# Retention groups of a decoder trunk: weight halves two products ahead, two weight sums by adding transfers, another order of groups

## The chip, the cores and the metric

The kernel runs on one core of one Trainium2 chip. TensorE (PE) multiplies matrices, VectorE (DVE) and ScalarE (ACT) do the elementwise work, GpSimd (POOL) a few small operations and some transfers, SyncE (SP) issues most transfers. The metric is the device time of one execution in microseconds (us), as a median of runs; lower is better.

## The reference

A trunk of two layers over 16 meta tokens and 512 tokens of width 1024, all in float32: a retention mixer, a SwiGLU FFN, a gated DeltaNet mixer, a second FFN, with RMS norms before each and a last one. The change lies in the retention mixer, which for each of 4 heads (key width 256, value width 512) computes

```
proj = h @ w_in;  q, k, v, g = split(proj)
q, k = rope(q), rope(k) / 16
scores = (q k^T) * decay mask of the head      (causal, all earlier tokens)
o = scores v
o = o * rsqrt(mean(o^2) + eps) * gn_w * silu(g)
out = concat(o) @ w_out
```

The kernel uses no chunks: it forms the scores of all 528 positions against the meta tokens (padded to 96 rows) and against four tiles of 128 tokens.

## The kernel before, in words

Every float32 product is made of three matmuls of a faster format: an operand is split into a high half (`whi`, a rounding copy on ScalarE) and a low half (`wlo`, a subtraction on VectorE), and `mm3` multiplies high by high, high by low and low by high. All its matmuls carry L407 in the profile, the splits L397/L398 (in `split`) or L170/L171 (in `load_w`).

The projections of head 0's queries and keys and of the gates of heads 0 and 1 are plain products. The other nine projections, named (head, kind) with the kinds QK, V and G, are done as Strassen groups in `quad`: seven products in place of eight, each of 24 matmuls on one of seven prepared combinations of the activations (`forms`: b11, t1, t2, b22, t3, b21, t4; names `fhb`, `fht`, `flb`, `flt` in the profile) and one of seven combinations of the weight blocks. `quad_part` makes the weight combination that the next product needs: it adds blocks on VectorE (L264, four additions per group), loads block "22" a second time, and splits the result. The loads (L257) go through four buffers `wraw`, the halves through three buffers `whi` and `wlo` each. The results are taken out of two PSUM pairs by `taken` (L287 to L304): three of the seven on VectorE, the others on ScalarE. Its destination is one of three row tiles: `at` and `bt` (in the buffer `xlo`) and `ct` (in the buffer `h`, as `oraw`, the attended output).

Beside the groups runs the work of the heads. `rope` rotates queries and keys (L530) with the tile `at` as its scratch; `ret_scores` makes masked scores (L582, L601); `ret_values` transposes values (L618, L626) and splits them; `ret_attend` multiplies (L644, L656), squares and scales (L660 to L665); `row_rsqrt` gives the norm's factor, with a power on POOL (L497) between two small sets of matmuls. `normed` (L781) applies it, `gated` (L800) multiplies by the gate and splits. Finished heads and gates wait in DRAM (`d_o`, `d_sg`) and are reloaded at the end.

The order of the work is written out by hand. A helper is a Python generator; `spawn(gen, delay)` queues it, and `tick()`, called after every second set of three matmuls of a group, runs those that are due. A `yield n` puts off the rest by n ticks, so that a group (28 ticks) interleaves with the helpers. `finish` runs a helper to its end at once. The framework that builds the program then gives each engine and each transfer queue one fixed order by priority and its own reckoning of when operands are there, which follows the written order mostly, not always. Each engine then works through its own queue in order.

The order of the heads is: (0,V); then for each head QK, V and, for heads 2 and 3, G. The rotation of a head is spawned after its QK group and so falls into the V group behind it, over about 16 ticks. After the last group, the three stored heads are gated and split, and the output projection (`w_ro`) starts with head 0.

Of the kernel before, what the change touches and what calls it, by code (L numbers as in the profile page):

```python
# [11 lines left out]
ALU = mybir.AluOpType  # L12
# [18 lines left out]
VT = 3  # L31
# [4 lines left out]
ROPED = 1  # L36
# [14 lines left out]
class Hybrid:  # L51
# [196 lines left out]
    def quad_begin(self, w):  # L248

        q = {"w": w, "raw": {}, "parts": []}  # L250
        for i, n in enumerate(self.BLOCKS):
            self.quad_fetch(q, n, i)
        return q

    def quad_fetch(self, q, n, i):
        q["raw"][n] = self.t(self.wp, [P, 1024], "wraw", bufs=RAW)
        self.nc.sync.dma_start(q["raw"][n], q["w"][i])  # L257

    def quad_part(self, q):

        raw = q["raw"]

        def add(dst, src):
            self.nc.vector.tensor_tensor(raw[dst], raw[dst], raw[src], op=ALU.add)  # L264

        n = len(q["parts"])
        if n in (1, 2, 3):
            add("22", ("21", "11", "12")[n - 1])
        if n == 4:
            add("21", "11")  # L270
            self.quad_fetch(q, "last", 2)
        src = ("11", "22", "22", "22", "21", "12", "last")[n]
        q["parts"].append(self.split_w(raw[src]))

    def quad(self, q, forms, hw, rows, following=None):
# [8 lines left out]
        nq = None  # L284
# [21 lines left out]
        for n, form in enumerate(self.FORMS):  # L306
            if n == 4 and following is not None:
                nq = self.quad_begin(following)
            if n < 6:
                self.quad_part(q)  # L310
            elif nq:
                self.quad_part(nq)
# [5 lines left out]
            for i in range(2):  # L318
                for k in range(4):
                    ws = slice(i * 512 + k * P, i * 512 + (k + 1) * P)  # L320
                    self.mm3(
                        [banks[i]],
                        (hi[:, ws], lo[:, ws]),
                        [(fh[:, k, :], fl[:, k, :])],
                        n in (0, 1, 5) and k == 0,
                        k == 3,
                        skip_group_check=True,
                    )
                    if k % 2:
                        self.tick()  # L330
            taken(n)
# [143 lines left out]
    def row_rsqrt(self, pool, acc, n, out):  # L475
# [27 lines left out]
        for j in range(4):  # L503
            nc.tensor.matmul(  # L504
                pr[:, j * P : (j + 1) * P], rc[:, j + 1 : j + 2].to_broadcast([P, P]), self.ident, start=True, stop=True
            )
        rb = self.t(pool, [P, T], "rb")
# [12 lines left out]
    def rope(self, qk, rows, tmp, cosr, sinr):  # L520
# [3 lines left out]
        r4 = rows.rearrange("p (n s) t -> p n s t", n=2)  # L524
        t1, t2 = r4[:, :, 0, :], r4[:, :, 1, :]
        x1, x2 = tmp[:, 0:2, :], tmp[:, 2:4, :]
        cos, sin = (c.unsqueeze(1).to_broadcast([P, 2, T]) for c in (cosr, sinr))
# [4 lines left out]
        tt(x1, t1, cos)  # L532
        yield ROPE
        tt(x2, t2, sin)
        yield ROPE
        tt(x1, x1, x2, ALU.subtract)
        yield ROPE
        self.split(hi[:, :, 0, :], lo[:, :, 0, :], x1)
        yield ROPE
        tt(t1, t1, sin)  # L540
        yield ROPE
        tt(t2, t2, cos)
        yield ROPE
        tt(t1, t1, t2, ALU.add)
        yield ROPE
        self.split(hi[:, :, 1, :], lo[:, :, 1, :], t1)

    def spread(self, dst, src):
# [5 lines left out]
        )  # L554

    def ret_scores(self, rp, dp, hd, q, k, km, out):
# [12 lines left out]
        for c0, c1 in ((NM, T), (0, NM)):  # L569
            yield 1  # L570
            nn = c1 - c0
            ps = self.psum_m()
            for s in range(2):
                self.mm3(
                    [ps[:96, :nn]],
                    (km[0][:, s, :], km[1][:, s, :]),
# [3 lines left out]
                )  # L580
            sc = self.t(dp, [P, T], "sc")
            nc.vector.tensor_tensor(sc[:96, :nn], ps[:96, :nn], dm[:96, c0:c1], op=ALU.mult)  # L582
            nc.scalar.copy(pm[:96, c0:c1], sc[:96, :nn])
            nc.vector.tensor_tensor(
                pm[64:96, c0:c1], sc[64:96, :nn], pm[64:96, c0:c1].bitcast(F32), op=ALU.subtract
            )
        for j in range(4):
            yield 1
            c0 = NM + j * P
            nn = T - c0  # L590
            ps = self.psum_m()
            for s in range(2):
                self.mm3(
                    [ps[:, :nn]],
                    (k[0][:, s, c0 : c0 + P], k[1][:, s, c0 : c0 + P]),
                    [(q[0][:, s, c0:], q[1][:, s, c0:])],
                    s == 0,
                    s == 1,
                )
            sc = self.t(dp, [P, T], "sc")  # L600
            nc.vector.tensor_tensor(sc[:, :nn], ps[:, :nn], dr[:, :nn], op=ALU.mult)  # L601
            hi = self.t(rp, [P, nn], f"ph{j}", F32R)
            lo = self.t(rp, [P, nn], f"pl{j}", F32R)
            self.split(hi, lo, sc[:, :nn])
            pj.append((hi, lo))
        out["pm"], out["pj"] = pm, pj

    def ret_values(self, rows, v3):
# [4 lines left out]
        def by_token(v):  # L613
# [3 lines left out]
            for j in range(4):  # L617
                nc.tensor.transpose(ps[:, j * P : (j + 1) * P], vt[:, NM + j * P : NM + (j + 1) * P], self.ident)  # L618
            c = slice(v * P, (v + 1) * P)
            self.split(vhi[:, :, c], vlo[:, :, c], ps.rearrange("p (j i) -> p j i", i=P))  # L620
            yield 1

        def meta():
            ps = self.psum_m()
            for v in range(4):
                nc.tensor.transpose(ps[:96, v * P : (v + 1) * P], self.vms[:, v, :], self.ident)  # L626
            nc.scalar.copy(vm[:96], ps[:96])
            nc.vector.tensor_tensor(vm[32:64], ps[32:64], vm[32:64].bitcast(F32), op=ALU.subtract)
            yield 1
# [1145 lines left out]
```

## Time and profile before

| | |
|---|---|
| time, median of 3 runs | 1730.27 us (1729.78 to 1732.37) |
| profiled run's own time | 1732.23 us |
| its span, first to last instruction | 1730.5 us |
| mean granted TensorE clock | 0.989 |
| busy: PE / weight loads / DVE / ACT / POOL | 98% / 91% / 70% / 50% / 4% |
| group stage | 82 to 368 us of the span |

Busy shares are over the whole span, and stages differ. A matmul's end is modelled and matmuls overlap, so idle time of PE in a stretch, its count of matmuls and the granted clock say more than its share. In a row of waits stand the total in us, the number of waits and the longest; "A <- B" means that A waited for B. Rows of work carry the line, the engine, output <- inputs by the names of the tiles, and shapes as partitions x elements.

### The profile page before, as it was taken

Reading aid. Unit: us, or ns where it says so; the run is one execution under the profiler, and the core shown is the slowest. Engines: PE = TensorE matmul, PEld = TensorE weight load, DVE = VectorE, ACT = ScalarE, POOL = GpSimd, SP = SyncE. Lnnn points to the kernel's source line nnn. Section 1 sums busy time; section 2 is a strip of 40 time slices with the busy share of each in tenths; the row PEclk is TensorE's granted clock in tenths of the full one; section 3 lists DMA queues with packets and bytes.
Section 4 is the critical chain, followed back from the end, with each engine's and each line's share of the span. In section 5 each row is a group of like instructions: output and inputs, shape, how many; then the busy total and the mean of one; then the engine's idle time right before and its main releaser. Section 6 shows DMA issues by size and latency. Waiting matters only on the chain.

```text
span 1730.5 us, 30404 instructions
## 1 busy us (share of the span) xinstructions
PE 1692.9 (98%) x12455; PEld 1576.7 (91%) x12455; DVE 1211.8 (70%) x1830; ACT 857.1 (50%) x1524; POOL 75.8 (4%) x130
## 2 busy tenths in 40 slices
PE   9999989899999999999999999999999999999997
PEld 9998989899999999999999978797977789999886
DVE  7868787873498887533688776685858798887322
ACT  5554454452355545422565536665666555555322
POOL 1000000000000000000030000000001000000010
PEclk9999999999999999999999999999999999999999
DMA  6333234472313332332264462433322223333231
GB/s 216 135 97 121 87 109 136 137 249 96 110 62 100 110 110 81 101 91 94 82 210 158 131 182 88 149 100 111 112 87 86 86 85 111 98 110 103 94 98 49
DMA packets 84524, 197.72 MB, mean 114 GB/s; under 512 B 19888, under 2 KB 37472, under 8 KB 83104
## 3 DMA queue, kind: packets, MB, share of 16 engines
q1 hardware_dynamic: 77056, 193.13, 34.2%
q10 hardware_dynamic: 6960, 1.84, 0.5%
q8 instruction: 98, 1.61, 0.4%
q0 software_dynamic: 368, 0.80, 0.1%
q14 instruction: 42, 0.34, 0.1%
HBM read 171.41 MB, written 24.33 MB: 113 GB/s over the span
## 4 chain that ended last, share of the span: by engine, by line
PE 81%; DVE 9%; issue 5%; ACT 2%; DMA 1%; POOL 1%; SPq 0%; POOLq 0%; ACTq 0%; DVEq 0%
PE g L407 64%; PE m L407 13%; DVE wlo L398 2%; DVE wraw L264 1%; DMA wraw<-in_w_ret_dram 1%; DVE xlo L530 1%; ACT whi L397 1%; DVE xhi L398 1%; DVE wlo L171 1%; PE m L504 1%; POOL ss L1435 0%; DVE ra L1022 0%; PE m L491 0%; PE m L1171 0%; PE m L1347 0%
## 5 line engine op out<-in xcount | busy, mean ns | idle before, releaser
L171 DVE TENSOR_TENSOR wlo<-wraw,whi 128x1024 fp32r<-128x1024 f32 (+1 forms) x140 | 166.4, 1191 | 177.6 <-ACT whi L170 175.4
L170 ACT CAST whi<-wraw 128x1024 fp32r<-128x1024 f32 (+1 forms) x140 | 143.2, 1024 | 260.9 <-PE g L407 141.5
L407 PE MATMUL g<-fht,whi 128*128 128x264 f32 (+1 forms) x864 | 247.7, 287 | 13.1 <-ACT xlo L291 13.0
L407 PE MATMUL g<-xhi,whi 128*128 128x264 f32 (+1 forms) x1024 | 255.0, 314 | 0.1
L407 PE MATMUL g<-xhi,wlo 128*128 128x264 f32 (+1 forms) x1024 | 248.4, 307 | 2.0 <-DVE wlo L171 2.0
L407 PE MATMUL g<-xlo,whi 128*128 128x264 f32 (+1 forms) x1024 | 248.5, 307 | 0.1
L407 PE MATMUL g<-fht,wlo 128*128 128x264 f32 (+1 forms) x864 | 245.2, 284 | 0.6 <-DVE wlo L398 0.6
L407 PE MATMUL g<-flt,whi 128*128 128x264 f32 (+1 forms) x864 | 245.7, 284 | 0.0
L397 ACT CAST whi<-wraw 128x1024 fp32r<-128x1024 f32 x129 | 135.1, 1050 | 122.2 <-issue 55.2
L407 PEld LDWEIGHTS g<-xhi,wlo 128*128 128x128 f32 x1024 | 166.6, 189 | 10.9 <-DVE wlo L171 2.2
L398 DVE TENSOR_TENSOR wlo<-wraw,whi 128x1024 fp32r<-128x1024 f32 x129 | 156.6, 1219 | 28.3 <-ACT whi L397 28.1
L407 PEld LDWEIGHTS g<-xhi,whi 128*128 128x128 f32 x1024 | 166.7, 190 | 10.6 <-issue 0.7
L407 PEld LDWEIGHTS g<-fht,whi 128*128 128x128 f32 x864 | 163.6, 189 | 13.9 <-ACT xlo L291 13.6
L407 PEld LDWEIGHTS g<-xlo,whi 128*128 128x128 f32 x1024 | 167.0, 190 | 7.3 <-DVE xlo L461 0.6
L407 PEld LDWEIGHTS g<-fht,wlo 128*128 128x128 f32 x864 | 162.6, 188 | 0.9 <-DVE wlo L398 0.9
L407 PEld LDWEIGHTS g<-flt,whi 128*128 128x128 f32 x864 | 162.8, 188 | 0.0
L407 PE MATMUL g<-fhb,whi 128*128 128x264 f32 (+1 forms) x432 | 123.1, 285 | 0.0
L407 PE MATMUL g<-fhb,wlo 128*128 128x264 f32 (+1 forms) x432 | 122.6, 284 | 0.5 <-DVE wlo L398 0.5
L407 PE MATMUL g<-flb,whi 128*128 128x264 f32 (+1 forms) x432 | 122.6, 284 | 0.0
L398 DVE TENSOR_TENSOR wlo<-wsum,whi 128x1024 fp32r<-128x1024 f32 x54 | 66.1, 1225 | 44.0 <-ACT whi L397 44.0
L397 ACT CAST whi<-wsum 128x1024 fp32r<-128x1024 f32 x54 | 56.6, 1049 | 58.5 <-PE m L407 23.7
L407 PEld LDWEIGHTS g<-fhb,wlo 128*128 128x128 f32 x432 | 81.2, 188 | 0.7 <-DVE wlo L398 0.7
(454 smaller groups left out, 3904.8 us busy)
## 6 DMA issues: line engine op xcount, KB each, us to landing
wraw<-in_w_gu_dram SPq DMA_DIRECT2D x66, 512.0 KB, 3.2
wraw<-in_w_ret_dram SPq DMA_DIRECT2D x56, 512.0 KB, 3.4
wraw<-in_w_d_dram SPq DMA_DIRECT2D x38, 512.0 KB, 3.5
sraw<-in_w_gu_dram SPq DMA_DIRECT2D x22, 512.0 KB, 3.5
wraw<-in_w_ro_dram SPq DMA_DIRECT2D x16, 512.0 KB, 4.0
wraw<-in_w_dqk_dram SPq DMA_DIRECT2D x16, 512.0 KB, 3.4
wraw<-in_w_dv_dram SPq DMA_DIRECT2D x16, 512.0 KB, 3.9
wraw<-in_w_dg_dram SPq DMA_DIRECT2D x16, 512.0 KB, 3.3
```

Of the source, the lines that this page charges most:

```text
L170: nc.scalar.copy(hi[:, c], raw[:, c])
L171: nc.vector.tensor_tensor(lo[:, c], raw[:, c], hi[:, c].bitcast(F32), op=ALU.subtract)
L264: self.nc.vector.tensor_tensor(raw[dst], raw[dst], raw[src], op=ALU.add)
L397: self.nc.scalar.copy(hi, src)
L398: self.nc.vector.tensor_tensor(lo, src, hi.bitcast(F32), op=ALU.subtract)
L407: mm(o, l, r[which], start=first and n == 0, stop=last and n == 2, **kw)
L504: nc.tensor.matmul(pr[:, j * P : (j + 1) * P], rc[:, j + 1 : j + 2].to_broadcast([P, P]), self.ident, start=True, stop=True)
L530: nc.vector.tensor_tensor(o, x, y, op=op)
```

## The change

What it does, part by part:

- Weight halves are made two products ahead: `quad_split` for product n + 2 is traced in the middle of product n (before: `quad_part` for product n right before it). The last two of a group make the first two of the next.
- Two of the weight sums are made by transfers: "22" + "21" (named "s") and "21" + "11" (named "s3") are loaded plainly by SP and then added to by a POOL transfer with `accum_op`. Two VectorE additions per group stay. A group has seven transfers (before: five), issued one by one at products 0 to 4.
- The groups come in the order (1,QK), (0,V), (2,G), (2,QK), (1,V), (3,QK), (2,V), (3,V), (3,G). The scores of head 0 fall into the first group; each head's values, attend step, norm and the next head's scores form one helper, `head`.
- `rope` works on one of queries and keys and one half at a time, in tiles of 528 columns (`ra`), and is drawn out over 33 ticks, more than one group.
- Short steps: in scores, values, attend and norm, matmuls, ScalarE's and VectorE's parts are put into ticks of their own.
- At the end the reloaded heads go one after the other through `bt` and `ct`, and their halves into the buffers of the forms and of the last queries and keys, which are free by then. The pool of the end and its own tiles are gone.

The diff, cut to its core:

```diff
-VT = 3
+VT = 1
-ROPED = 1
+ROPED = (1, 6)
+GATED = 10
...
+    PARTS = ("11", "s", "s", "s", "s3", "12", "22")
+
+    def quad_fetch(self, q, n):
+        q[n] = self.t(self.wp, [P, 1024], "wraw", bufs=RAW)
+        first, then = {"11": (0, None), "s": (2, 1), "s3": (1, 0), "12": (3, None), "22": (2, None)}[n]
+        self.nc.sync.dma_start(q[n], q["w"][first])
+        if then is not None:
+            self.nc.gpsimd.dma_start(q[n], q["w"][then], accum_op=ALU.add)
+
+    def quad_sum(self, q, n):
+        if n in (2, 3):
+            self.nc.vector.tensor_tensor(q["s"], q["s"], q[("11", "12")[n - 2]], op=ALU.add)
+
+    def quad_split(self, q, n):
+        q["parts"].append(self.split_w(q[self.PARTS[n]]))
+
+    def quad_start(self, w):
+
+        q = {"w": w, "parts": []}
+        for n in ("11", "s", "s3", "12"):
+            self.quad_fetch(q, n)
+        for n in range(2):
+            self.quad_split(q, n)
...
-            if n == 4 and following is not None:
-                nq = self.quad_begin(following)
-            if n < 6:
-                self.quad_part(q)
-            elif nq:
-                self.quad_part(nq)
+            pq, pn = (q, n + 2) if n < 5 else (nq, n - 5)
+            if pq:
+                self.quad_sum(pq, pn)
+            if n == 0 and nq:
+                self.quad_fetch(nq, "s")
...
+                if i == 0 and pq:
+                    self.quad_split(pq, pn)
+                    if n == 1:
+                        self.quad_fetch(q, "22")
+                    if nq and 2 <= n <= 4:
+                        self.quad_fetch(nq, ("11", "s3", "12")[n - 2])
...
+        for i in range(2):
+            t1, t2 = rows[:, 2 * i, :], rows[:, 2 * i + 1, :]
+            for half in range(2):
+                x, y = (self.t(self.tp, [P, T], "ra", bufs=4) for _ in range(2))
+                tt(x, t1, (cosr, sinr)[half])
+                yield ROPE
+                tt(y, t2, (sinr, cosr)[half])
+                yield ROPE
+                tt(x, x, y, (ALU.subtract, ALU.add)[half])
+                yield ROPE
+                nc.scalar.copy(hi[:, i, half, :], x)
+                yield 1
+                tt(lo[:, i, half, :], x, hi[:, i, half, :].bitcast(F32), ALU.subtract)
+                yield ROPE - 1
...
+        yield from self.together([(i, g) for i, g in enumerate((meta(NM, T), meta(0, NM), *map(tile_, range(4))))])
...
+        return self.together([(VT + v, by_token(v)) for v in range(4)] + [(VT + 4, meta())])
...
-        quads = [(0, V), (1, QK), (1, V), (2, QK), (2, V), (2, G), (3, QK), (3, V), (3, G)]
+        quads = [(1, QK), (0, V), (2, G), (2, QK), (1, V), (3, QK), (2, V), (3, V), (3, G)]
...
+        def head(hd, rows, made=None, first=None):
+
+            assert hd == 0 or "acc" in orow[hd - 1]
+            yield from self.ret_values(rows, v3)
+            if first:
+                self.finish(first)
+            yield from self.ret_attend(v3, sc[hd], oraw, orow[hd])
+            gens = [(0, normed(hd))]
+            if made:
+                gens.append((0, scores(hd + 1, made)))
+            yield from self.together(gens)
...
+        done = self.spawn(scores(0, {"gen": (), "qk": qk}), 1)
+        product(ct)
+        self.finish(done)
+        made = turn(ct)
+        product(at)
+        done = self.spawn(head(0, at, made))
+        gate(bt)
+        nc.sync.dma_start(d_sg[2], bt)
+        self.finish(made["gen"])
+        product(ct)
+        self.finish(done)
+        made = turn(ct)
+        product(at)
+        done = self.spawn(head(1, at, made))
+        product(bt)
+        made = turn(bt, done)
+        product(at)
+        done = self.spawn(head(2, at, made))
+        product(ct)
+        done = self.spawn(head(3, ct, None, done))
+        early = self.spawn(gated(0, bt, ct, ("b11", "t1")), GATED)
+        gate(at)
+        self.finish(done)
+        self.finish(early)
+        for hd, names in ((1, ("t2", "b22")), (2, ("t3", "b21"))):
+            self.finish(gated(hd, bt, ct, names))
+        self.finish(gated(3, oraw, at, None))
```

`together` is new: it merges several generators by their due ticks into one. `turn` spawns a rotation, after the helper `first` where one is given.

More of the change, by code (lines that the diff above doesn't have):

```diff
@@ L554, in spread, with together @@
         )
+    @staticmethod
+    def together(gens):
+        left = [(d, i, g) for i, (d, g) in enumerate(gens)]
+        heapq.heapify(left)
+        now = 0
+        while left:
+            due, i, g = heapq.heappop(left)
+            if due > now:
+                yield due - now
+                now = due
+            for delay in g:
+                heapq.heappush(left, (now + delay, i, g))
+                break
     def ret_scores(self, rp, dp, hd, q, k, km, out):
@@ L728, in retention @@
             self.finish(rows)
-            self.finish(self.rope(qk, keep, temp, cosr, sinr))
+            self.finish(self.rope(qk, keep, cosr, sinr))
         self.late_consts()
@@ L804, in retention @@
-        orow, steps, attend = attended(*scored(0))
-        for hd in range(1, RH):
-            qk = qk_tiles()
-            turned = roped(hd)
-            if hd < 3:
-                self.finish(attend)
-                stored(hd - 1, orow)
-            orow, steps, attend = attended(*scored(hd, turned))
-            if hd > 1:
-                if hd == 3:
-                    first = qk_tiles()
-                    def reload():
-                        for step in steps:
-                            self.finish(step)
-                        nc.sync.dma_start(at, d_o[0])
-                        nc.sync.dma_start(ct, d_sg[0])
-                        yield RELOAD
-                        gated(0, at, ct, *first)
-                    reloaded = self.spawn(reload(), TO_ATTEND)
-                gate(hd)
-                self.finish(attend)
-                if hd == 2:
-                    stored(hd, orow)
@@ L829, in retention @@
-        self.finish(reloaded)
-        inner.close()
-        sgs = self.t(self.xp, [P, KT, T], "xhi")
-        for i in range(2):
-            nc.sync.dma_start(sgs[:, 4 * i : 4 * i + 4, :], d_sg[i + 1])
-        op = self.pool(ctx, "reto", 1)
-        o = {0: [tuple(s[:, v // 2, v % 2, :] for s in first) for v in range(4)]}
-        raws = [None, at, self.t(op, [P, 4, T], "oraw"), oraw]
-        for hd in (1, 2):
-            nc.sync.dma_start(raws[hd], d_o[hd])
-        for kt in range(4, KT):
-            nc.sync.dma_start(self.h[:, kt, :], a["hT"][kt])
@@ new lines, in scores, with turn @@
+        def scores(hd, made):
+            self.finish(made["gen"])
+            parts = [[t_[:, i] for t_ in made["qk"]] for i in range(2)]
+            yield from self.ret_scores(rp, dp, hd, *parts, km, sc[hd])
+        def turn(rows, first=None):
+            made = {}
+            def run():
+                if first:
+                    self.finish(first)
+                made["qk"] = qk_tiles()
+                yield from self.rope(made["qk"], rows, cosr, sinr)
+            made["gen"] = self.spawn(run(), ROPED[first is not None])
+            return made
@@ new lines, in gated @@
+        def gated(hd, raw, sg, names):
+            if names:
+                hi, lo = ([self.t(fo, [P, 2, T], f"f{s}{n}", F32R) for n in names] for s in "hl")
+            else:
+                hi, lo = ([t_[:, r] for r in range(2)] for t_ in qk_tiles())
+            o[hd] = [(hi[v // 2][:, v % 2, :], lo[v // 2][:, v % 2, :]) for v in range(4)]
+            if hd < 3:
+                nc.sync.dma_start(raw, d_o[hd])
+                nc.sync.dma_start(sg, d_sg[hd])
+            yield RELOAD
+            for r in range(2):
+                rs = raw[:, 2 * r : 2 * r + 2, :]
+                nc.vector.tensor_tensor(rs, rs, sg[:, 2 * r : 2 * r + 2, :], op=ALU.mult)
+                yield 1
+                nc.scalar.copy(hi[r], rs)
+                yield 1
+                nc.vector.tensor_tensor(lo[r], rs, hi[r].bitcast(F32), op=ALU.subtract)
```

208 lines of the change are left out of this document (78 added, 130 removed).

## Prediction

> **What bounds the kernel now.** I read the page first, then the stage that the change touches in stretches of 10 us, then the waits of TensorE, then VectorE's order of work inside one stall.
>
> ```profile
> span 1730.5 us, 30404 instructions
> PE 1692.9 (98%) x12455; PEld 1576.7 (91%) x12455; DVE 1211.8 (70%) x1830; ACT 857.1 (50%) x1524; POOL 75.8 (4%) x130
> ```
>
> TensorE is the bound, and the diff adds or removes no matrix product. So only time that TensorE loses can be won. The stage of the nine Strassen groups ("quads") runs from 82 to 368 us; columns of the next rows are length, then PE, PEld, DVE, ACT, POOL busy, granted clock, DMA share, GB/s.
>
> ```profile
> 82.00:368.00 286.00, 270.97 (x2036) 260.64 (x2035) 221.35 (x298) 141.72 (x215) 8.48 (x8) 0.96 0.37 127
> ...
> 70.00:80.00 10.00, 10.00 (x84) 10.00 (x83) 6.88 (x9) 2.93 (x4) 0.00 (x0) 1.00 0.25 87
> ...
> 140.00:150.00 10.00, 7.50 (x62) 7.29 (x60) 10.00 (x10) 2.52 (x4) 0.00 (x0) 1.00 0.11 42
> 150.00:160.00 10.00, 8.56 (x33) 6.89 (x34) 7.71 (x12) 5.01 (x6) 0.00 (x0) 0.66 0.17 52
> ...
> 210.00:220.00 10.00, 6.90 (x57) 6.69 (x55) 10.00 (x9) 3.12 (x4) 0.00 (x0) 0.97 0.04 18
> 220.00:230.00 10.00, 9.16 (x42) 7.70 (x43) 8.16 (x13) 4.41 (x6) 0.00 (x0) 0.69 0.22 59
> ...
> 300.00:310.00 10.00, 5.52 (x46) 5.31 (x44) 9.97 (x10) 3.00 (x5) 0.00 (x0) 0.91 0.17 52
> 310.00:320.00 10.00, 9.39 (x49) 8.07 (x50) 8.44 (x14) 4.57 (x7) 0.00 (x0) 0.75 0.53 179
> ```
>
> The whole stage loses 286.0 - 271.0 = 15.0 us idle and 0.04 x 271 = 10.8 us of clock, 25.9 us together: the most that can be won. Three pairs of stretches hold nearly all of it. Idle: 2.50 + 1.44 + 3.10 + 0.84 + 4.48 + 0.61 = 13.0 us. Clock: 8.56 x 0.34 + 6.90 x 0.03 + 9.16 x 0.31 + 5.52 x 0.09 + 9.39 x 0.25 = 8.8 us. Sum 21.8 us. In each of them VectorE has 10 of 10 us of work.
>
> ```profile
> PE g L407 <- ACT xlo L291: 13.0, 3, 5.1
> PE m L644 <- DVE vm L628: 1.9, 4, 0.8
> ```
>
> The 13.0 us are three waits for the same thing: ScalarE copying the first product of a V group out of PSUM (L291) into `at`. VectorE's queue shows why that copy is late:
>
> ```profile
> 141.39 1.22 DVE L264 TENSOR_TENSOR wraw<-wraw,wraw 128x1024 f32<-128x1024 f32 x1
> 142.53 1.25 DVE L530 TENSOR_TENSOR xlo<-h,cosr 128x1056 f32<-128x1056 f32 x1
> 143.70 1.25 DVE L530 TENSOR_TENSOR xlo<-h,sinr 128x1056 f32<-128x1056 f32 x1
> ...
> 148.37 1.22 DVE L264 TENSOR_TENSOR wraw<-wraw,wraw 128x1024 f32<-128x1024 f32 x1
> 149.51 1.25 DVE L398 TENSOR_TENSOR qklo<-xlo,qkhi 128x1056 fp32r<-128x1056 f32 x1
> 150.68 1.25 DVE L530 TENSOR_TENSOR h<-h 128x1056 f32<-128x1056 f32 x1
> 152.04 1.21 DVE L398 TENSOR_TENSOR wlo<-wraw,whi 128x1024 fp32r<-128x1024 f32 x1
> ```
>
> The rotation keeps its products in `xlo`, which here is `at` itself. The last read of them starts at 149.51 and ends at 150.76; only then may the copy write there. The rotation's eight operations come almost in one block, with no weight half made between 141 and 152. Starts in a row give what VectorE takes when saturated: 1.14 us for 1024 columns, 1.17 us for 1056.
>
> ```profile
> 151.00:153.00 2.00, 1.56 (x4) 1.17 (x5) 2.00 (x4) 1.43 (x2) 0.00 (x0) 0.53 0.58 221
> 153.00:155.00 2.00, 2.00 (x8) 1.61 (x7) 2.00 (x4) 0.03 (x1) 0.00 (x0) 0.50 0.00 0
> 155.00:157.00 2.00, 2.00 (x8) 1.45 (x7) 0.75 (x2) 1.32 (x2) 0.00 (x0) 0.50 0.00 0
> ```
>
> After the wait TensorE runs at a clock of 0.50 for some 6 us. So a wait of four to five us costs about seven.
>
> **The change, part by part.** Rows for the prices:
>
> ```profile
> L398 DVE TENSOR_TENSOR wlo<-wraw,whi 128x1024 fp32r<-128x1024 f32 x57 | 68.9, 1218 | 8.8 <-ACT whi L397 8.7
> L264 DVE TENSOR_TENSOR wraw<-wraw,wraw 128x1024 f32<-128x1024 f32 x32 | 38.9, 1218 | 3.2 <-DMA wraw<-in_w_ret_dram 2.9
> L618 PEld LDWEIGHTS m<-ident,xlo 128*128 128x128 f32 x64 | 7.5, 140 | 0.0
> ...
> 62.57 0.70 DVE L219 TENSOR_TENSOR dr<-sc,dr 128x528 f32<-128x528 f32 x1
> 63.19 0.70 DVE L216 SCALAR_TENSOR_TENSOR dm<-dm,sc 128x528 f32<-128x528 f32 x1
> 63.81 0.70 DVE L398 TENSOR_TENSOR flb<-sc,fhb 128x528 fp32r<-128x528 f32 x1
> ...
> wraw<-in_w_ret_dram SPq DMA_DIRECT2D x56, 512.0 KB, 3.4
> fnw<-in_fnw_dram POOLq DMA_DIRECT2D x1, 512.0 KB, 5.3
> xlo<-d_o SPq DMA_DIRECT2D x2, 1056.0 KB, 5.9
> xhi<-d_sg SPq DMA_DIRECT2D x2, 1056.0 KB, 7.4
> ...
> 1597.91 0.64 POOL L1582 DMA_DIRECT2D fnw<-in_fnw_dram  x1 [225.69 <-DVE hidl L398]
> 129.68 2.02 POOL L497 TENSOR_TENSOR rc<-rc,mhalf 128x5 f32<-128x5 f32 x1 [102.59 <-DVE rc L496]
> ```
>
> *Rotation.* Eight operations of 1056 columns (9.4 us) become sixteen of 528. Three in a row started 0.62 us apart, so 9.9 us: 0.5 us more work per head. The products go to small `ra` tiles, so the copy at L291 no longer waits for them, and the block is drawn out from about 16 steps to 33 (one step, or tick, is 6 matmuls). This removes the named wait: -21.8 us, if nothing else is late.
>
> *Weight sums.* Four VectorE additions per group become two: 18 fewer, 18 x 1.14 = 20.5 us of VectorE, worth nothing on the path by itself but it makes the next sum possible. In exchange each group has 7 transfers for 5, two of them adding, on POOL's queue behind their plain load.
>
> *What is late next: VectorE.* TensorE does 84 matmuls in 10 us, 0.119 us each; a product of 24 takes 2.86 us, a group 20.0 us, a step 0.714 us. VectorE per group: 7 halves and 2 sums at 1.14, two evacuations of 528 columns at 0.62, two of half that at about 0.4: 12.3 us. The V group that carries a rotation gets 14 of its 16 operations: 12.3 + 8.7 = 21.0 us against 20.0, so VectorE ends about 1.0 us behind. (With the four additions and the whole block it would be 14.6 + 9.4 = 24.0.) Operands two products ahead leave 1.5 x 2.86 = 4.3 us for ScalarE's and VectorE's halves, about 2.3 us, so 1.0 us behind stops no product. It comes out at the attend step: its first matmul (L644) needs VectorE's last value half (L628), traced just behind it. Up to there, 9 steps: TensorE 9 x 0.714 + 5 transposes of four at 7.5/16 = 0.47, 8.8 us; VectorE 9/28 of a group, two rotation operations, five value halves and four small copies, 4.0 + 1.2 + 3.1 + 0.5 = 8.8. The 1.0 us stays, for heads 0 and 1. The third rotation starts later, and five of its operations fall into these steps instead of two: 1.9 us more, 2.9 for head 2. I take 2.9 for head 3 too, where the scaling and scores of head 2 run into the same steps. Together 7.8 us, for the 1.9 us that L644 waits today: +5.9 us. Bounds: -1.9 (no wait left) and +13.0 (the old idle comes back whole).
>
> *Adding transfers.* No row shows one. Below: 5.3 us, the plain POOL transfer of the same shape. Above: 5.3 + 7.4 = 12.7, as if the second reading cost as much as the slowest 1056 KB reload. I take 8, nearer the plain row, since shape and queue are the same. "s" is fetched at product 0 and split in the middle of product 6, 6.5 x 2.86 = 18.6 us later; less 3.4 us of plain load, 15.2 us are left, so both bounds are hidden: 0. Cover lost from 15.2 on. The other loads keep three or four products, over 8.6 us for 3.4.
>
> *POOL's queue.* Behind a waiting adding transfer stands the power operation (2.02 us) of the row norm, for which TensorE waits. It is traced near step 25 of a group, the transfers at steps 0 and 14 with 3.4 us (5 steps) for their load and 0.64 us of issue, so they have passed: 0. If they meet each time, 4 x 3.4 = 13.6 us.
>
> *The end.* Heads 1 and 2 are reloaded one behind the other into the same two tiles: at most 7.4 us of load and 6 operations of 1.17 each. The first can start some 8 steps before the last group ends; head 2's operands are then there by about 2 x (7.4 + 4.7) - 5.7 = 18.5 us, when TensorE, with 48 matmuls (5.7 us) per unit of output weights and two units per head, reaches them at 22.8. Cost 0; without the early start 1.4 us.
>
> Sum: -21.8 + 5.9 = -15.9. Span 1730.5 - 15.9 = 1714.6; 1.7 us lie around it (profiled run 1732.23), and that run is 2.0 us above the median 1730.27. Against the median: 1714.4, **1714**.
>
> **The rivals.** *A: VectorE's backlog takes the wait's place.* Rotation operations stand ahead of weight halves and TensorE waits for `wlo`, as the empty stretch from 141 to 152 suggests; against it, 21.0 us of work for 20.0. Price: the 13.0 us stay in shorter pieces, the half clock goes: -8.8, 1721.5. It decides once VectorE falls more than the 4.3 - 2.3 = 2.0 us behind that the two products of lead allow.
> [...]
>
> *B: POOL's queue*, the 13.6 us above: -2.3, 1728. For it: POOL waits in order; against: the steps lie apart.
>
> *C, slower: adding transfers too slow.* Two per group share POOL's queue; a group has (286 - 25.9)/9 = 28.9 us. At 16 us each they need 32, 3.1 us per group for eight groups, 25 us: 1739. It decides from (28.9 + 15.9/8)/2 = 15.4 us on. Against it: 5.3 us for the plain row, a third of that; for it: nothing here shows the addition's price.
> [...]
>
> *D: nothing won.* The build's own ordering packs the rotation into a block again and one wait of the old size returns at `wlo`: 1730.
>
> **How the numbers follow.** Forecast 0.50 (its own range 1706 to 1722), A 0.20, B 0.08, C 0.15, D 0.07. About 0.2%, 3.5 us, is what a measurement of this kernel tells from no change. Faster: forecast, A and half of B, 0.74; same: D and the other half, 0.11; slower: C, 0.15. The range goes from 1703 (the whole 25.9 us and 1 us of unseen gaps) to 1729 (B); C and D's upper part stay out.
>
> **What would show it.** Right: no wait on L291's successor, no stretch at 0.50 between 82 and 350 us, VectorE's additions in the stage halved, adding transfers landing under 13 us, the row norm's power operation still within 1 us of its input, L644 waits of 1 to 3 us. Wrong: TensorE waits for `wlo` or `whi` (A), for `rc` (B), VectorE or ScalarE waits for a transfer into `wraw` (C), or a gap at the start of the output projection.

## The result, and the profile after

The changed kernel takes 1713.88 us (median; 1711.89 to 1718.1) where the kernel before takes 1730.18 (1729.78 to 1732.37): a ratio of 0.9901, 95% interval 0.9889 to 0.9914, or 16.3 us. 1714 was forecast. The experiments below show that the sum came out right over two errors that largely cancelled (a backlog priced at 5.9 us that did not come, and 4.1 us that were not priced), so that part of the closeness is luck, and that the cause named for its largest term was only half of a pair.

The page of the profiled execution (its own time is 1718.1 us, the slowest of the four):

```profile
span 1716.3 us, 30519 instructions
PE 1687.9 (98%) x12455; PEld 1575.2 (92%) x12455; DVE 1193.9 (70%) x1848; ACT 854.8 (50%) x1532; POOL 89.1 (5%) x148
```

TensorE has the same 12455 matmuls, so again only lost time can differ. Stretches of the changed kernel (length, then PE, PEld, DVE, ACT, POOL busy, granted clock, DMA share, GB/s):

```profile
40.00:50.00 10.00, 7.63 (x60) 7.42 (x60) 10.00 (x17) 6.38 (x10) 0.00 (x0) 0.97 0.28 102
50.00:60.00 10.00, 10.00 (x74) 10.00 (x73) 8.56 (x15) 2.85 (x4) 0.00 (x0) 0.86 0.48 157
...
82.00:352.00 270.00, 267.90 (x2080) 260.76 (x2079) 209.63 (x314) 144.77 (x226) 20.29 (x24) 1.00 0.56 165
```

The group stage now ends near 352 us, loses 270.0 - 267.9 = 2.1 us and runs at a clock of 1.00; it lost 15.0 us and 10.8 us of clock before. But there is a new hole ahead of it, at 40 to 60 us, where TensorE of the kernel before is busy 20.00 of 20 us at a clock of 1.00. TensorE's waits name it:

```profile
PE g L414 <- DVE ra L775: 2.4, 1, 2.4
...
PE m L674 <- DVE vm L658: 1.5, 2, 1.1
```

The 13.0 us for the copy out of PSUM are gone. L674 is the attend step (L644 before). L775 takes a gate's product out of PSUM; VectorE's order in front of it is shown with the experiment on head 0's rotation below. After it TensorE ran at half clock for 3.4 us, from 49.4 to 52.8 us (rows in the last section).

A landmark shows what the mixer as a whole won: the FFN's first weight load (`sraw`; the numbers are instruction time as least, median and most in ns, then first and last start). Before:

```profile
L339 SPq DMA_DIRECT2D sraw<-in_w_gu_dram x11: 327/328/426, 461.6 to 647.6; - x11
```

and after:

```profile
L346 SPq DMA_DIRECT2D sraw<-in_w_gu_dram x11: 327/328/425, 443.8 to 630.3; - x11
```

461.6 - 443.8 = 17.8 us are won by then. Some of that is lost again behind it in code that neither version touches: 1.5 us by the medians, 3.6 in this profiled execution (span 14.2 us shorter). The landmark is used below wherever medians are too coarse; it comes from one execution of each kernel.

The transfers of the weight blocks, KB each and median us from issue to landing:

```profile
wraw<-in_w_ret_dram SPq DMA_DIRECT2D x56, 512.0 KB, 4.1
...
wraw<-in_w_ret_dram POOLq DMA_DIRECT2D x18, 512.0 KB, 5.5
```

The adding transfers land in 5.5 us. VectorE's queue in the first V group with a rotation (start, duration):

```profile
109.57 1.22 DVE L405 TENSOR_TENSOR wlo<-wraw,whi 128x1024 fp32r<-128x1024 f32 x1
110.71 0.70 DVE L535 TENSOR_TENSOR ra<-ra,ra 128x528 f32<-128x528 f32 x1
111.33 1.21 DVE L263 TENSOR_TENSOR wraw<-wraw,wraw 128x1024 f32<-128x1024 f32 x1
112.46 0.70 DVE L535 TENSOR_TENSOR qklo<-ra,qkhi 128x528 fp32r<-128x528 f32 x1
113.08 0.70 DVE L535 TENSOR_TENSOR ra<-h,sinr 128x528 f32<-128x528 f32 x1
113.72 1.23 DVE L405 TENSOR_TENSOR wlo<-wraw,whi 128x1024 fp32r<-128x1024 f32 x1
```

Rotation operations (L535) stand between weight halves (L405) and sums (L263), where before VectorE made no low half from 141 to 152 us.

### The profile page after: what moved, and what is told of

It is laid out like the page before. It is cut to its first block, busy times and chain, and to the rows that moved or that the text cites. A ratio compares the mean times of both kernels' runs of the same rounds, so it can differ in the third digit from the quotient of the medians.

```text
span 1716.3 us, 30519 instructions
## 1 busy us (share of the span) xinstructions
PE 1687.9 (98%) x12455; PEld 1575.2 (92%) x12455; DVE 1193.9 (70%) x1848; ACT 854.8 (50%) x1532; POOL 89.1 (5%) x148
## 4 chain that ended last, share of the span: by engine, by line
PE 69%; DVE 8%; issue 5%; ACT 2%; POOL 1%; DMA 0%; ACTq 0%; POOLq 0%; DVEq 0%
PE g L414 54%; PE m L414 11%; DVE wlo L405 1%; DVE ra L1062 1%; DVE wlo L172 1%; DVE wsum L212 1%; POOL ss L1475 0%; ACT whi L404 0%; DVE flt L405 0%; PE m L1211 0%; PE m L1387 0%; DVE flb L405 0%; DMA wraw<-in_w_ret_dram 0%; ACT whi L171 0%; PE m L1330 0%
## 5 line engine op out<-in xcount | busy, mean ns | idle before, releaser
L414 PE MATMUL g<-fht,whi 128*128 128x264 f32 (+1 forms) x912 | 256.6, 286 | 0.0
L414 PE MATMUL g<-fht,wlo 128*128 128x264 f32 (+1 forms) x912 | 254.9, 284 | 0.8 <-DVE wlo L405 0.8
L414 PE MATMUL g<-flt,whi 128*128 128x264 f32 (+1 forms) x912 | 254.4, 283 | 0.0
L405 DVE TENSOR_TENSOR wlo<-wraw,whi 128x1024 fp32r<-128x1024 f32 x129 | 157.3, 1220 | 32.2 <-ACT whi L404 31.6
L414 PEld LDWEIGHTS g<-flt,whi 128*128 128x128 f32 x912 | 170.7, 189 | 0.2
L414 PEld LDWEIGHTS g<-fht,wlo 128*128 128x128 f32 x912 | 169.7, 188 | 1.0 <-DVE wlo L405 1.0
L414 PE MATMUL g<-fhb,whi 128*128 128x264 f32 (+1 forms) x480 | 134.1, 288 | 0.0
L414 PE MATMUL g<-fhb,wlo 128*128 128x264 f32 (+1 forms) x480 | 132.6, 284 | 0.6 <-DVE wlo L405 0.5
L414 PE MATMUL g<-flb,whi 128*128 128x264 f32 (+1 forms) x480 | 132.0, 283 | 0.0
L405 DVE TENSOR_TENSOR wlo<-wsum,whi 128x1024 fp32r<-128x1024 f32 x54 | 66.1, 1225 | 44.3 <-ACT whi L404 44.3
L414 PEld LDWEIGHTS g<-fhb,wlo 128*128 128x128 f32 x480 | 88.5, 188 | 1.0 <-DVE wlo L405 1.0
L414 PEld LDWEIGHTS g<-flb,whi 128*128 128x128 f32 x480 | 89.1, 189 | 0.1
```

Source lines behind the costliest of these rows:

```text
L405: self.nc.vector.tensor_tensor(lo, src, hi.bitcast(F32), op=ALU.subtract)
L414: mm(o, l, r[which], start=first and n == 0, stop=last and n == 2, **kw)
```

## The experiments

All times in us; "sraw" is the landmark, from each profiled execution. Every kernel computes the whole result. The ratio is to the kernel before on the same chip, with its 95% interval.

| kernel | median | ratio | sraw |
|---|---|---|---|
| before | 1730.2 to 1731.6 | 1 | 461.6 |
| changed, again | 1715.46 | 0.9904 [0.9890, 0.9917] | 443.7 |
| changed, first rotation wide | 1711.66 | 0.9885 [0.9869, 0.9900] | 440.7 |
| before, scratch moved | 1731.06 | 0.9999 [0.9990, 1.0008] | 460.0 |
| changed, four sums on VectorE | 1713.44 | 0.9896 [0.9882, 0.9909] | 443.0 |
| changed, rotations in a block | 1723.94 | 0.9957 [0.9945, 0.9968] | 453.8 |
| changed, one product ahead | 1711.10 | 0.9883 [0.9870, 0.9895] | 439.8 |
| first rotation wide, a step more | 1715.26 | 0.9909 [0.9894, 0.9925] | 445.2 |
| before, drawn out over 16 steps | 1726.17 | 0.9970 [0.9958, 0.9981] | 453.6 |
| order, drawing out, short steps | 1711.52 | 0.9886 [0.9871, 0.9900] | 440.5 |
| changed, 16 steps | 1714.04 | 0.9901 [0.9887, 0.9914] | 442.2 |
| first wide, one product ahead | 1709.78 | 0.9877 [0.9861, 0.9894] | 438.7 |
| changed, block, one ahead, four sums | 1734.51 | 1.0013 [1.0004, 1.0023] | 462.6 |

**The changed kernel again.** No edit.

> The changed kernel once more, on the chip of the runs beside it. Both theories: a ratio of 0.990 (1713 us), a stage of the groups without a stretch at half clock between 85 and 350 us, and the wait of about 2.4 us for the gate's evacuation at 45 to 48 us again. If that wait is missing here, the theory that the first rotation costs 4 us falls.

Measured 1715.46 (1712.61 to 1716.03). The 2.4 us wait for L775 is there again, and so is half clock after it.

**Head 0's rotation wide again.**

```diff
-            self.finish(self.rope(qk, keep, cosr, sinr))
+            self.finish(self.rope_wide(qk, keep, temp, cosr, sinr))
```

`rope_wide` holds the eight operations of before, with a scratch tile of its own.

> The changed kernel, with the rotation of head 0 alone (ahead of the groups) back in its eight operations of 1056 columns. My theory: the sixteen narrow operations hold back the gate's evacuation by 2.6 us, TensorE waits 2.4 us for it and then runs some 3 us at half clock; so 3 to 5 us come back against the changed kernel: 1708 to 1710 us where it has 1713, and no stretch under a clock of 0.9 between 46 and 54 us. Rival (the order of the scores and gates ahead of the stage costs it, whatever the form): within 1 us of the changed kernel, the half clock stays.

1711.66, 3.8 us less than the changed kernel beside it; by the landmark 3.0. The hole is gone:

```profile
40.00:50.00 10.00, 9.98 (x81) 9.63 (x80) 10.00 (x15) 7.08 (x10) 0.00 (x0) 1.00 0.47 150
50.00:60.00 10.00, 10.00 (x80) 9.58 (x79) 10.00 (x18) 4.97 (x9) 0.00 (x0) 1.00 0.37 120
```

So it is the first rotation's new form that costs 3 to 4 us, not the order of scores and gates around it. It does so in a roundabout way. VectorE's queue in the changed kernel:

```profile
41.34 0.70 DVE L535 TENSOR_TENSOR qklo<-ra,qkhi 128x528 fp32r<-128x528 f32 x1
...
46.60 0.70 DVE L405 TENSOR_TENSOR flb<-sc,fhb 128x528 fp32r<-128x528 f32 x1
47.22 1.31 DVE L775 TENSOR_TENSOR ra<-g,rb 128x528 f32<-128x528 f32 x2
```

and with the rotation wide:

```profile
45.40 0.70 DVE L803 TENSOR_TENSOR ra<-g,rb 128x528 f32<-128x528 f32 x1
...
46.19 0.71 DVE L405 TENSOR_TENSOR flb<-dm,fhb 128x528 fp32r<-128x528 f32 x1
```

The narrow rotation is done at 42.04, earlier than the wide one (45.48). But the framework's order then puts a weight half and seven operations that prepare the activations (three at L405, two at L220, one each at L212 and L217) ahead of the gate's evacuation; with the wide form the evacuation (L803 there) stands ahead of the first at L405. Why the order turns out so wasn't followed up.

**The kernel before with the scratch alone moved.** This is the test of the cause that the prediction named.

```diff
-            return self.spawn(self.rope(qk, ct, at, cosr, sinr), ROPED)
+            return self.spawn(self.rope(qk, ct, bt, cosr, sinr), ROPED)
```

> The kernel before, with one name changed: the rotation keeps its products in the third row tile instead of the one that the V group's first product is copied into. Block, order, four additions stay. Theory 1 (the overwritten tile is the whole cause): the three waits of 13.0 us for the copy and the half clock go, most of 21.8 us comes back: 1709 to 1715 us. Theory 2 (VectorE's backlog would have held TensorE anyway, since that group needs 24.0 us of VectorE in 20): TensorE waits for weight halves (wlo) instead, at most 9 us come back: 1721 to 1730 us.

1731.06: nothing by the medians, and 1.6 us by the landmark. The theory of the overwritten tile as the whole cause falls; theory 2's waits for weight halves came, and cost more than it said. The waits for the copy (13.0 us) went, and others of 9.8 us took their place in the stage:

```profile
PE g L407 <- ACT whi L397: 6.5, 2, 3.3
PE g L407 <- DVE wlo L398: 3.3, 1, 3.3
```

VectorE's queue, and ScalarE's below it, show why:

```profile
142.79 1.25 DVE L530 TENSOR_TENSOR xlo<-h,cosr 128x1056 f32<-128x1056 f32 x1
...
147.46 1.25 DVE L530 TENSOR_TENSOR h<-h,cosr 128x1056 f32<-128x1056 f32 x1
148.63 1.22 DVE L264 TENSOR_TENSOR wraw<-wraw,wraw 128x1024 f32<-128x1024 f32 x1
```

```profile
144.87 0.60 ACT L291 COPY xlo<-g 128x528 f32<-128x528 f32 x1 [2.19 <-PE g L407]
...
149.94 1.05 ACT L397 CAST whi<-wraw 128x1024 fp32r<-128x1024 f32 x1 [0.57 <-DVE wraw L264]
```

The copy now starts at 144.87. But the next product's high half is made from a weight sum (L264) that stands behind five rotation operations, is done at 149.85, and the half at 150.99; TensorE resumes at 151.04. In the kernel before, ScalarE's queue had both locks already:

```profile
149.68 1.04 ACT L397 CAST whi<-wraw 128x1024 fp32r<-128x1024 f32 x1 [0.77 <-DVE wraw L264]
150.79 0.60 ACT L291 COPY xlo<-g 128x528 f32<-128x528 f32 x1
```

The high half was there at 150.72 and the copy at 151.39, 0.67 us later. The profile named the later one, and opening it shortened the wait by those 0.67 us, from 3.94 to 3.27. The second place is the same (3.94 to 3.27); in the third a low half ended 1.8 us ahead of the copy, and the wait went from 5.09 to 3.30. TensorE still ran at half clock after each of the three (for 6.84 us after the first, last section).

**The weight sums back on VectorE.**

```diff
-            self.nc.gpsimd.dma_start(q[n], q["w"][then], accum_op=ALU.add)
+            pass
-        if n in (2, 3):
-            self.nc.vector.tensor_tensor(q["s"], q["s"], q[("11", "12")[n - 2]], op=ALU.add)
+        if n in (1, 2, 3):
+            self.nc.vector.tensor_tensor(q["s"], q["s"], q[("s3", "11", "12")[n - 1]], op=ALU.add)
+        if n == 2:
+            self.nc.vector.tensor_tensor(q["s3"], q["s3"], q["11"], op=ALU.add)
```

At the start of the stage one sum more is made in the same way.

> The changed kernel without the adding transfers: all four weight additions of a group on VectorE again, five transfers. My theory (the saving matters, because a V group with a rotation has 21.0 us of VectorE work to 20.0 of TensorE): 2.3 us more per group put it 3.3 us behind, over the 2.0 us that two products of lead allow, and TensorE waits for wlo, in three groups 1 to 3 us each and 1.5 to 3 us more at each attend step: 6 to 15 us slower than the changed kernel. Rival (the transfers only take work off an engine that has the time): within 2 us of it.

1713.44 and 443.0: no loss against the changed kernel's 1715.46 and 443.7. My expectation of 6 to 15 us was wrong. The one wait for `wlo` in the stage is 0.6 us. The profiled execution escaped the half clock at 50 us (1.7 us, last section), so the sums may cost it some 1 us by the landmark. With the rotations drawn out, the adding transfers are worth next to nothing.

**The rotations of heads 1 to 3 in a block.**

```diff
-                yield from self.rope(made["qk"], rows, cosr, sinr)
+                self.finish(self.rope(made["qk"], rows, cosr, sinr))
+                yield 1
```

> The changed kernel with the sixteen rotation operations of heads 1 to 3 issued in one block of 9.9 us again (scratch in its small tiles, operands two products ahead, two sums by transfers). With the scratch moved alone, TensorE waited 3.3 to 3.8 us per block for weight halves and ran at half clock after it. If the block is what must go (theory 1), the same waits return here: 12 to 20 us slower than the changed kernel. If the second product of lead does it (theory 2), a lead longer by one product of 2.86 us leaves 0.5 to 1 us of wait per block and no half clock: 1 to 4 us slower.

1723.94, some 8.5 us slower than the changed kernel, 10.1 by the landmark; between the two expectations.

```profile
PE g L414 <- DVE wlo L405: 8.5, 8, 2.7
```

7.1 us of these lie in the stage, where the changed kernel has none. So drawing out is worth some 10 us to a kernel that has the lead and the transfers. The block is looser than it is written: the first one takes VectorE from 107.27 to 122.26, 15.0 us for 9.9 us of rotation, because weight halves and sums still get in between.

**Halves one product ahead.**

```diff
-            pq, pn = (q, n + 2) if n < 5 else (nq, n - 5)
+            pq, pn = (q, n + 1) if n < 6 else (nq, 0)
```

and the five places where loads are issued, moved by one product; at the start of the stage one half is made ahead in place of two.

> The changed kernel with the weight halves made one product ahead of use. The rotation stays drawn out. Theory 2 (the lead does it): a half is issued in the middle of the product before, 1.43 us ahead, and takes 2.3 us on ScalarE and VectorE; where VectorE is full (three V groups) each of 7 products waits 0.9 us or more, so 19 us or more slower than the changed kernel. Theory 1 (the drawn-out rotation does it): within 3 us of it.

1711.10 and 439.8: no loss, if anything 4 us won (1.7 of it the half clock, which this execution escaped, and 1.4 the waits at L674, which it doesn't have). My expectation of 19 us or more was wrong, and the reason is in the order of the queues. TensorE's rows:

```profile
118.11 0.29 PE L414 MATMUL g<-fhb,whi 128*128 128x264 f32 x1
...
121.04 0.29 PE L414 MATMUL g<-fht,whi 128*128 128x264 f32 x1
...
123.96 0.29 PE L414 MATMUL m<-fhb,whi 128*128 128x264 f32 x1
```

and VectorE's:

```profile
118.05 1.22 DVE L405 TENSOR_TENSOR wlo<-wraw,whi 128x1024 fp32r<-128x1024 f32 x1
...
119.81 1.22 DVE L405 TENSOR_TENSOR wlo<-wraw,whi 128x1024 fp32r<-128x1024 f32 x1
```

Products begin at 118.11, 121.04 and 123.96. The two low halves end at 119.27 and 121.03, and by the order of the parts they are those of the second and the third: 1.8 and 2.9 us ahead of use. The later one is written in the middle of the second product, near 122.5, and is done before that product begins. So the framework's order puts halves ahead of the place where they are written, and the written lead of 1.43 us isn't the real one.

**One step between the value halves and the attend products.** On the kernel with the wide first rotation:

```diff
             yield from self.ret_values(rows, v3)
+            yield 1
```

> The changed kernel with head 0's rotation wide, as in the run that took 1711.7 us, and one step of six matmuls between the value halves and the attend products of every head. Theory (TensorE waits 1.9 us in two places for the last value half because the attend products stand directly behind it): these waits go, 1 to 2 us faster than the run with the wide rotation alone, 1710 us. Rival (the wait moves to the next operand): no difference.

1715.26 (1712.63 to 1720.15), slower than the 1711.66 without it. The waits for `vm` did fall, from 1.9 to 0.9 us, but a new one appears, TensorE's for the row norm:

```profile
PE m L508 <- POOL rc L505: 3.7, 1, 3.7
```

It was not queued: POOL had been idle for 30 us. The power operation itself was slow:

```profile
343.45 4.33 POOL L505 TENSOR_TENSOR rc<-rc,mhalf 128x5 f32<-128x5 f32 x1 [30.45 <-DVE rc L504]
```

In the changed kernel's second run the same one took:

```profile
345.45 2.04 POOL L505 TENSOR_TENSOR rc<-rc,mhalf 128x5 f32<-128x5 f32 x1 [29.06 <-DVE rc L504]
```

Why it took twice as long is open. The wait of 3.7 us outweighs the 1.0 us won. Whether the added step brings the slow operation was not shown: one execution was profiled, and the runs spread over 7.5 us.

**The kernel before, scratch moved and rotation drawn out over 16 steps.**

```diff
-SCORES = (12, 3)
+SCORES = (12, 18)
-            return self.spawn(self.rope(qk, ct, at, cosr, sinr), ROPED)
+            return self.spawn(self.rope(qk, ct, bt, cosr, sinr), ROPED)
```

> The kernel before with two edits: the scratch tile moved, as in the run that took 1731.1 us, and the scores of heads 1 to 3 started at step 18 instead of 3, so that the rotation's eight operations stand two steps apart in place of in one block. One product of lead, four additions on VectorE and the order of the groups stay. Theory 1 (the block held the weight halves back): the group needs 24.0 us of VectorE in 20.0, so it ends some 4 us behind in pieces under 1 us, without half clock: 13.0 + 8.8 less 3 x 4 are 10 us won, 1718 to 1722 us. Theory 2 (one product of lead is too short whatever the order): TensorE waits for wlo at most products of these groups, 1727 us or more.

1726.17, 4.6 us won, 8.0 by the landmark: less than theory 1 said, more than theory 2. TensorE waits often and shortly, which would fit an engine that is too full:

```profile
PE g L407 <- ACT whi L397: 5.8, 6, 1.7
PE g L407 <- DVE wlo L398: 1.9, 3, 0.8
```

In the order of before there is little room to draw the rotation out further, since scores and attend step of the same head must follow within that V group; no longer form of it was tried.

**Order, drawing out and short steps alone.** The three edits above together: first rotation wide, one product ahead, four sums on VectorE.

> The changed kernel with three parts undone together: head 0's rotation wide, weight halves one product ahead, all four additions on VectorE. What is left is the order of the groups, the narrow rotations in small tiles drawn over 33 steps, and the short steps. Theory 3 (these alone carry the gain; each of the two others alone made no difference): 1708 to 1712 us. Theory 4 (lead and transfers stand in for each other: with both gone VectorE's 23.3 us for 20.0 meet a lead of one product): waits for wlo of 1 to 3 us in each of three groups, 1715 us or more.

1711.52, as good as the changed kernel with the wide first rotation (1711.66). Theory 3 holds: lead and transfers are not needed. Waits for `wlo` in the stage are three, 2.1 us together:

```profile
PE g L416 <- DVE wlo L407: 2.1, 3, 0.8
```

**Sixteen steps instead of 33.**

```diff
-ROPE = 2
+ROPE = 1
```

> The changed kernel with the rotation's operations of heads 1 to 3 one step apart in place of two: 16 steps (11.4 us) in place of 33. VectorE then has 9.9 us of rotation and 7.0 us of other work in 11.4 us, 5.5 us behind at the end, against some 8 us for the whole block. If the length is what counts: 4 to 9 us slower than the changed kernel, waits of 1 to 2.5 us for wlo. Rival (any distance between the operations is enough): within 2 us of it.

1714.04 and 442.2, against 1713.88 and 1715.46, 443.8 and 443.7 of the changed kernel; the profiled execution escaped the half clock at 50 us (1.7 us). So it is the same, and my expectation of 4 to 9 us failed. The written distance isn't the real one here either: VectorE's sixteen operations of head 1 run from 106.38 to 126.58, 20 us and not 11.4, and from 107.86 to 133.87 in the changed kernel. With lead and two sums 20 us were enough; whether 26 are needed without them wasn't tried.

**First rotation wide and one product ahead.** Both edits from above.

> The changed kernel with head 0's rotation wide and weight halves one product ahead (adding transfers stay). If the two gains add (1711.7 and 1711.1 us alone, for 1715.5 and for its like): 1707 to 1709 us, no wait over 1 us between 30 and 350 us. Rival (both only show the scatter of the changed kernel): 1711 us or more.

1709.78 (1708.39 to 1713.04), between the two expectations, the fastest median and 5.7 us under the changed kernel's second. The intervals of the two ratios (0.9861 to 0.9894 and 0.9890 to 0.9917) still touch; what stands on the traces of it is the 3 us of the first rotation. In the stage it has two waits for `vm`, 1.0 us together, and no half clock.

**Block, one product ahead, four sums.** What is left of the change is the order, the small scratch tiles and the short steps.

> The changed kernel with the rotations of heads 1 to 3 in one block, halves one product ahead and four additions on VectorE: what is left is the order of the groups, the scratch tiles and the short steps. If the two-product lead and the saved additions were what made the block cost less (1723.9 us) than in the kernel before with the scratch moved (1731.1 us): 1728 to 1733 us, waits of over 3 us for wlo or whi and half clock after them. Rival (the order of the groups made that difference): 1722 to 1726 us.

1734.51, slower than the kernel before. With the 2.4 us that the narrow first rotation costs here taken off, it is the kernel before within 1 us.

```profile
PE g L416 <- DVE wlo L407: 11.2, 6, 5.2
PE g L416 <- ACT whi L406: 3.4, 1, 3.4
```

Beside the block with lead and transfers this says that those two are worth some 10 us where the block stands (10.6 by medians on two chips, 8.8 by the landmark). Which of the two wins it wasn't separated.

So there are two ways out of the same loss. Drawing the rotation out over more than a group recovers nearly all of it, on top of the new order, the small tiles and the short steps, which win nothing with the block left (1734.51). That it needs the new order is argued from the room it takes: in the old order the most that was tried won 4.6 us. The second product of lead with the two transfers recovers about half with the block left. Together they give no more than drawing out alone.

## Why the prediction was right, and where not

**The bound and the most that can be won** (25.9 us in the stage): held. 17.8 us were won by the landmark, 4.1 were lost ahead of the stage, and 2.1 are left in it: 24.0 of the 25.9 are accounted for. The clock's 10.8 us in that bound rest on a rounded 0.96 and are good to 1.4 us. Of the stretches that the prediction lists, VectorE has 10 of 10 us of work in the first of each pair only, not in each of them (7.71, 8.16 and 8.44 us in the others).

**The rotation, -21.8 us.** The size came out, the cause was half wrong. The prediction read the wait for the copy as an effect of the scratch tile alone, "removes the named wait: -21.8 us, if nothing else is late". Something else was late by only 0.7 us less in two places and 1.8 us less in the third: weight halves behind the same block. Moving the scratch alone shortened 13.0 us of waits to 9.8 and won nothing by the medians. The change also draws the block out, which the prediction counted within the same step, so its sum didn't suffer. The stretch from 141 to 152 us, which I put down as an argument for rival A, was the second cause. It was empty of low halves only: ScalarE made a high half in it, at 149.68, late for want of its sum.

The prediction and the text ahead of it also say that the old rotation was spread over some 16 steps. Its operations are written so, but the scores, due 3 steps into the group, finish the rotation at once: it was one block, as the profile showed.

**VectorE's backlog at the attend step, +5.9 us.** This term failed. It took 1.0, 1.0, 2.9 and 2.9 us of wait for the last value half. Measured: two waits, 1.5 us together, for 1.9 before: -0.4. The prediction added up work against time within one group, 21.0 for 20.0, as if no half could be made earlier. With 23.3 us of work (four sums on VectorE) TensorE waited 0.6 us for weight halves, and with one product of lead as well 2.1. In the trace halves run ahead of their written place (one product ahead, above).

**A term that was missing: the first rotation, +4.1.** The prediction costed the narrow form at "0.5 us more work per head" and looked at the three heads in the groups only. Head 0's rotation stands ahead of them, issued at once, and in its new form a gate's evacuation comes behind operations that it used to precede: 2.4 us idle and 1.7 us of half clock, which not every execution has. With these two, -21.8 - 0.4 + 4.1 = -18.1, against the 17.8 measured. The backlog was 6.3 us too dear and the first rotation 4.1 too cheap: that they nearly cancel is luck.

**Adding transfers, 0.** Right: 5.5 us where 8 was taken and 15.2 could be covered. Their saving, "makes the next sum possible", was not needed: 18 fewer additions on VectorE and no time won by it.

**POOL's queue, 0.** Right: the power operations start when their input is there, and TensorE has no wait for `rc`. **The end, 0.** Right: TensorE is busy without a gap from 350 to 380 us. Its working has a slip: six operations at 1.17 us are 7.0 us, not the 4.7 that were added, which gives 23.1 us where TensorE comes at 22.8, a cost of 0.3 us.

**The rivals.** A's place was right and its condition wrong: the backlog at `wlo` does come where the block stays, at more than A's price (1731.1 with the scratch moved), and near it with lead and transfers (1723.9). In the changed kernel it doesn't come. That shorter pieces bring no half clock, on which A's price of 1721.5 rests, was the author's estimate: in the kernel before, drawn out, one wait of 1.67 us was followed by it. B and C did not come. D is what the block without lead and transfers shows: 1734.5, the old waits back at `wlo`.

## What to carry to other kernels

A wait is put down to what ended last. Before a gain is counted on it, find what would have ended next: here it ended 0.7 to 1.8 us earlier, and the named cause alone was worth nothing by the medians. A block of some 9 us on an engine that feeds TensorE every 3 us was better drawn out than outrun here: without lead and transfers, drawing out gave what all three gave together. When an operation gets a new form, every place that calls it counts, those outside the edited stage too.

## What the runs showed of the hardware

**The half clock came in portions of 3.4 us.** Stretches of 1 us of the changed kernel, around its wait from 45.60 to 47.97:

```profile
46.00:47.00 1.00, 0.00 (x0) 0.00 (x0) 1.00 (x3) 1.00 (x3) 0.00 (x0) 1.00 0.92 352
...
49.00:50.00 1.00, 1.00 (x8) 1.00 (x7) 1.00 (x2) 0.27 (x1) 0.00 (x0) 0.71 0.53 201
50.00:51.00 1.00, 1.00 (x7) 1.00 (x6) 1.00 (x3) 0.00 (x0) 0.00 (x0) 0.50 0.45 167
51.00:52.00 1.00, 1.00 (x6) 1.00 (x6) 1.00 (x3) 0.63 (x1) 0.00 (x0) 0.50 1.06 296
52.00:53.00 1.00, 1.00 (x7) 1.00 (x6) 1.00 (x3) 0.63 (x1) 0.00 (x0) 0.58 0.84 307
```

The clock's loss is 0.29 + 0.50 + 0.50 + 0.42 = 1.71 us, that is 3.42 us at half clock, and it began 1.4 us after the wait was over. The kernel before with the scratch moved, after 3.27 us idle (147.76 to 151.04):

```profile
150.00:151.00 1.00, 0.00 (x0) 0.00 (x0) 1.00 (x2) 0.99 (x1) 0.00 (x0) 0.70 0.16 33
151.00:152.00 1.00, 0.81 (x2) 0.50 (x2) 1.00 (x2) 0.00 (x0) 0.00 (x0) 0.50 0.77 246
...
157.00:158.00 1.00, 1.00 (x7) 0.79 (x5) 0.00 (x0) 0.94 (x1) 0.00 (x0) 0.88 0.00 0
```

With five more rows of 0.50 between 152 and 157 the loss is 0.30 + 6 x 0.50 + 0.12 = 3.42 us: 6.84 us at half clock, twice the portion.

**A short wait was followed by it in some executions and not in others.** The same wait of 2.4 us for L775 was followed by half clock in the changed kernel, in its second run and with the rotations in a block, and not in four others: four sums, one product ahead, 16 steps, and the last experiment. The first of these, in rows:

```profile
46.00:47.00 1.00, 0.00 (x0) 0.00 (x0) 1.00 (x3) 1.00 (x2) 0.00 (x0) 1.00 0.83 250
...
50.00:51.00 1.00, 1.00 (x10) 1.00 (x9) 1.00 (x3) 0.00 (x0) 0.00 (x0) 1.00 0.33 116
```

The last experiment has a clock of 1.00 in each row from 44 to 56 us too. A wait of 1.67 us, shortly after other short ones, was followed by it (the kernel before, drawn out, at 151.55 us: its matmuls start 0.22 us apart from 154.43 to 157.51, 0.12 apart ahead of the wait); one of 1.66 us in the same execution (at 218.32), one of 1.96 us in the kernel before (1033.50 to 1035.46) and one of 2.70 us (the block) were not. Every wait of 3.27 us or more in the stage of the kernel before (3.94, 3.94 and 5.09 us), with the scratch moved (3.27, 3.27 and 3.30) and in the last experiment (5.20, 3.96 and 3.35) was followed by it. In the kernel before the half clock begins three times in the stage:

```profile
151.00:152.00 1.00, 0.56 (x2) 0.50 (x2) 1.00 (x3) 0.43 (x2) 0.00 (x0) 0.56 0.81 299
...
219.00:220.00 1.00, 0.00 (x0) 0.00 (x0) 1.00 (x1) 0.92 (x1) 0.00 (x0) 0.69 0.00 0
...
308.00:309.00 1.00, 0.00 (x0) 0.00 (x0) 1.00 (x2) 0.07 (x1) 0.00 (x0) 0.56 0.00 0
```

A mean clock of 0.56 in the row means that 0.88 us of it were at half clock, so it began at 151.12; in the same way 219.38 and 308.12. That is 3.62, 2.48 and 2.61 us after TensorE fell idle (at 147.50, 216.90 and 305.51); in the changed kernel it is 3.82 us after (45.60 to 49.42). The distances between the three, 68.26 and 88.74 us, are 20 and 26 times 3.413 us. Behind the stage the changed kernel's half clock begins at 1018.80, 1035.88 and 1326.00:

```profile
1018.00:1019.00 1.00, 1.00 (x7) 1.00 (x8) 0.43 (x3) 1.00 (x2) 0.00 (x0) 0.90 1.11 412
1035.00:1036.00 1.00, 1.00 (x5) 0.60 (x4) 0.36 (x1) 0.94 (x3) 0.00 (x0) 0.94 0.08 25
1326.00:1327.00 1.00, 1.00 (x4) 0.77 (x3) 1.00 (x2) 0.33 (x1) 0.00 (x0) 0.50 0.00 0
```

These distances, 17.08 and 290.12 us, are 5 and 85 times 3.413. So in these two executions the starts lie whole portions apart. It isn't idle time alone that brings it, as the profile shows idle time: from 1032 to 1035 us, ahead of the second of these starts, TensorE is busy 1.00 of 1 us in each row, and so it is from 1044 to 1048 us in the kernel before, where the half clock begins at 1048.82. What decides was not shown.

Whether it comes is worth 1.7 us to a kernel that keeps the 2.4 us wait, and it acts behind the landmark too: there the changed kernel's profiled execution has 13.7 us at half clock up to 1340 us, the one before 10.2, which is 1.7 of the 3.6 us lost again. Part of the scatter of the changed kernel's runs may be this, which the profiles of single executions don't settle.
